# A hybrid decoder layer: four recurrent weight pairs as seven products, one scan a half, and a re-ordered out-projection

## The chip, the cores and the metric

The kernel runs on one core of a Trainium2 chip. The metric is device time in microseconds (us), the median of several executions. The engines are named as in the profile: PE (TensorE, matrix products; PEld loads its weights), DVE (VectorE), ACT (ScalarE), POOL (GpSimd) and SP (SyncE, which issues most DMAs). [...]

## The reference, cut to what matters

One layer of a decoder, 1024 tokens of 1024 features in float32. The part that the change touches, shortened:

```python
u = rms_norm(h, norm1_g)
aq, ak, av, hq, hf, hi, hg = split(u @ w_in)               # seven blocks of 512 columns
attn = rms_norm(dilated_attention(aq, ak, av), attn_norm_g)
# recurrence, 4 heads of 128: f gate, cumulated log gate per chunk, running state
forget = lb + (1 - lb) * sigmoid(f); key = 1 - forget
b = cumsum(log(forget), over the chunk)
q_dec = silu(q) * exp(b); k_inv = key * exp(-b)
o = tril(q_dec k_inv^T) iv + q_dec state;   state = exp(b_end) * state + (key * exp(b_end - b))^T iv
rec = rms_norm(o, hgrn_norm_g) * silu(hg)
h = h + concat(attn, rec) @ w_out                          # the out-projection
h = h + conv_glu(rms_norm(h, norm2_g)); out = rms_norm(h, final_norm_g)
```

## The kernel before

Feature rows lie on the 128 partitions and tokens along the free dimension, in two halves of 512 tokens. Every large product is done in split float32: an operand is a high part (a cast to the 32-bit format that PE reads fast) and a low part (the rest), and `three` (L493 to L495) issues three matmuls of 128 x 512 for each 128 x 128 block of weights: high by high, high by low, low by high.

Weights come through a `Ring`. A plan lists the pieces of weights in their order of use; each is loaded by SP into one of five raw buffers, cast by ACT (L87, `whi`) and subtracted by DVE (L89, `wlo`). At most five split pieces are alive; when a product has used one, `done` fetches the next of the plan.

The order of PE's work is written out by hand. The instructions of the other engines are ordered by a planner, from what they wait for and are wanted for, except where `pin` or `order` keeps them in program order. The hand-written order weaves two streams: dense products stand in a queue, `fill`, as generators, each of which gives 0.65 of credit for three matmuls; the recurrence, the attention and the norms call `fill.run(x)` to have x of credit of dense matmuls issued before their own next step. In the recurrent stage `play` does this by a list of `steps`, each with a due time in units of 5.2 of credit.

There are 12 recurrent weight blocks (hq, hf and hg, four heads each), taken as six pairs in the list `HG`, with both token halves. The first pair, (hf 0, hq 0), is done early, in the attention stage, as seven products instead of eight: `PairMix` forms sums of the four weight pieces on DVE, `pair_block` (L508 to L536) runs seven products of four blocks on sums of the operand (the tiles B11, B21, B22, T1 to T4) and puts their results together on DVE, with two alternating PSUM banks, "mm". Its results go to DRAM. Afterwards `restore` rebuilds the plain operand in T4's place, from x. The five other pairs are plain: `hg_block` runs for both halves and both blocks `plain_product`, 8 blocks of 3 matmuls, and `scaled` (L837) multiplies the result by the norm's factor R1.

`f_out`, `q_out` and `g_out` apply the sigmoid gates: a maximum on DVE, three ACT passes (L826 to L828), a product on DVE. `f_out` also computes B and the logarithm A (L845, L846). `recur` is one head and one half, in five steps: the scans of log gates, four of 128 columns (L935), small copies into `sm`, exponentials and products on DVE (L944 to L948); the transposes psK and the scores psA; psU and the chain of states U (L972 to L982); psO and its norm (L992 to L1001); psT and the product with the gate (L1007 to L1009). `attn_stat` and `attn_parts` norm and split the attention's output; `split_rec` splits the recurrence's.

The out-projection has, for each of the 8 blocks d of 128 output features and each half, an attention part (part 0) and a recurrent part (part 1) of four blocks each. For the first half, all the attention parts are done first, then all the recurrent parts (`out_half`); for the second half both parts of a block accumulate in one PSUM bank (`out_pair`). `square` adds up the squares for the next norm, `norm2` (L1157 on), on POOL; it is woven into the second half's products. Then the feed-forward part follows, which the change does not touch.

Of the kernel before, what the change touches and what calls it, by code (L numbers as in the profile page):

```python
# [28 lines left out]
NPAIR = 10  # L29
BIG = 1e30  # L30
# [219 lines left out]
def hybrid_kernel(ctx: ExitStack, tc: tile.TileContext, xT, w_qk, w_tok, w_hg, w_out, w_up,  # L250
# [17 lines left out]
    lb = cpool.tile([P, 96], F32, name="lb")  # L268
    epool = ctx.enter_context(pool("eps", "right"))
    eps_ = epool.tile([P, 120], F32, name="eps")  # L270
    epst, onehalf = eps_[:, 0:1], eps_[:, 64:65]
# [5 lines left out]
    R1T = rv.tile([P, P], F32, name="R1T")  # L277
    DVE.memset(ones, 1.0)
    DVE.memset(eps_[:, 0:64], EPS)
    DVE.memset(eps_[:, 64:120], 1.5)  # L280
# [21 lines left out]

    plan.extend((("V", c), tok(0, c // KS, c % KS)) for c in range(NCT))
# [4 lines left out]
    HG = [(("hf", 0), ("hq", 0)), (("hg", 0), ("hg", 1)), (("hf", 1), ("hq", 1)), (("hf", 2), ("hq", 2)),  # L308
          (("hf", 3), ("hq", 3)), (("hg", 2), ("hg", 3))]
    want_mix(HG[0], w_hg[4], w_hg[0], False)  # L310
    for pair in HG[1:]:
        for kind, h in pair:
            i = 4 * {"hq": 0, "hf": 1, "hg": 2}[kind] + h
            plan.extend((((kind, h), x), w_hg[i, :, x * H2 : (x + 1) * H2]) for x in range(2))

    def out_order(hf, d):

        return [(p, e) for p in range(2) for e in (d, d + 1)]

    def want_out(hf, d, part):  # L320
        plan.append(((("out", hf, d), part), w_out[d, :, part * H2 : (part + 1) * H2]))

    for part, d in ((x, d) for x in range(2) for d in range(NCT)):
        want_out(0, d, part)
    for d0 in range(0, NCT, 2):
        for part, d in out_order(1, d0):
            want_out(1, d, part)
# [121 lines left out]
    def rms1():  # L449
        st = bank("o", "sst")  # L450
        for hf in range(2):
            for i in range(4):
                PE.matmul(st[:, 4 * hf + i : 4 * hf + i + 1], sums[hf][:, i * P : (i + 1) * P], ones[:, 0:1], start=True, stop=True)
        tm = rv.tile([P, 64], F32, name="rst")
        rstd(R1T[:, 0:NCT], tm[:, 0:NCT], st[:, 0:NCT], 1.0 / DM)

# [203 lines left out]
    if True:  # L660
# [115 lines left out]
        def restore():  # L776
            for c in range(KS):
                x = mtile(f"x12_{c}")
                nc.sync.dma_start(x, xT[c, :, halves[1]])
                hi, lo = (y[:, c] for y in opn["T4"])  # L780
                ACT.mul(hi, x, col(V_G1 + c))
                DVE.scalar_tensor_tensor(lo, x, col(V_G1 + c), f32(hi), op0=ALU.mult, op1=ALU.subtract)

        def early_evac(m, hf, src):
            DVE.tensor_mul(src, src, R1[:, halves[hf]])
            nc.sync.dma_start(rawg[HG[0][m][0], hf], src)

        def early():

            yield from pair_block(HG[0], lambda m, hf: mtile(f"e{m}_{hf}"), early_evac)  # L790
            restore()
# [26 lines left out]
    with pool("hg", "right") as hg:  # L818
# [6 lines left out]
        def sigmoid(dst, src):  # L825
            ACT.activation(dst, src, AF.Exp, scale=-1.0)  # L826
            ACT.activation(dst, dst, AF.Ln, bias=1.0)
            ACT.activation(dst, dst, AF.Exp, scale=-1.0)  # L828

        gate, G, R2 = {}, {}, []  # L830

        def tile_of(kind, h, hf):
            tag, bufs = {"hf": ("A", 3), "hq": ("E", 4), "hg": ("GH"[h // 2], 4)}[kind]
            return ht(tag, f"{tag}{h}_{hf}", bufs)

        def scaled(x, hf, src):
            DVE.tensor_mul(x, src, R1[:, halves[hf]])  # L837
            return x

        def f_out(h, hf, A):  # L840
            B = ht("B", f"B{h}_{hf}", 3)
            DVE.tensor_scalar_max(A, A, -40.0)
            sigmoid(A, A)

            ACT.activation(B, A, AF.Identity, bias=lb[:, NG + h : NG + h + 1], scale=lb[:, 2 * NG + h : 2 * NG + h + 1])  # L845
            ACT.activation(A, A, AF.Ln, bias=lb[:, h : h + 1], scale=lb[:, NG + h : NG + h + 1])  # L846
            gate.setdefault((h, hf), {}).update(A=A, B=B)

# [7 lines left out]
        def g_out(h, hf, g_):  # L856
# [5 lines left out]

        OUT = {"hf": f_out, "hq": q_out, "hg": g_out}

        def hg_block(pair):

            for hf in range(2):
                for kind, h in pair:
                    ps = bank("mm", f"p{kind}{h}_{hf}")
                    yield from plain_product(ps, (kind, h), hf)  # L870
                    OUT[kind](h, hf, scaled(tile_of(kind, h, hf), hf, ps))

        ar = [ht("H", f"ar{x}", 4) for x in range(2)]
# [15 lines left out]
        def attn_parts(hf):  # L889
            hi, lo = spare(f"attn{hf}")  # L890
            for c in range(4):
                a = ht("F", f"as{hf}_{c}")
                nc.sync.dma_start(a, rawd[c, hf])
# [20 lines left out]
        for hf in range(2):  # L914
            for kind, h in HG[0]:
                x = tile_of(kind, h, hf)
                nc.sync.dma_start(x, rawg[kind, hf])
                OUT[kind](h, hf, x)

        AT = hg.tile([P, 4, P], F32, name="AT")  # L920
# [4 lines left out]
        def recur(h, hf):  # L925
            A, B, E = (gate[h, hf].pop(x) for x in "ABE")
            nm = f"{h}_{hf}"
            iv = hg.tile([P, 4, P], F32, tag="iv", name=f"iv{nm}", bufs=2)
# [4 lines left out]
            for c in range(4):  # L933
                s = slice(c * P, (c + 1) * P)
                DVE.tensor_tensor_scan(C[:, s], ones, A[:, s], 0.0, op0=ALU.mult, op1=ALU.add)  # L935
            sm = hg.tile([P, 12], F32, tag="sm", name=f"sm{nm}", bufs=2)
            DVE.tensor_copy(sm[:, 0:4], C3[:, :, 63])
# [679 lines left out]
```

## Time and profile before

| | |
|---|---|
| median of 3 runs | 1158.48 us (1157.97 to 1160.91) |
| the profiled execution, its own time | 1157.98 us |
| its span in the profile | 1156.2 us |
| PE busy | 1141.3 us, 6460 matmuls |
| DVE busy | 935.2 us, 1738 instructions |
| ACT busy | 572.2 us, 1121 instructions |
| attention stage with the query/key products and the early pair | about 95 to 266 us |
| the five plain recurrent pairs, with the recurrence | 266.1 to 405.8 us |
| out-projection | 405.8 to 505.4 us |
| feed-forward part and final norm | 505.4 to 1156.2 us |

A row of the timeline has the start and the length in us, the engine, the line of the kernel, the operation, what it writes and reads, its shape, and in brackets the idle time before it with what ended it. A row of a group has a count, then the busy time in us and the mean of one in ns, then the idle time before. A row of the waits has the time in all, how often and the longest. Matmuls are pipelined, so the start of the next, not the end of the last, gives what one costs.

### The profile page before, as it was taken

The numbers are of one execution on the slowest core, as the hardware profiler recorded it, in microseconds if no ns is written. First come the engines' busy times: TensorE is split into PE (matmuls) and PEld (weight loads), VectorE is DVE, ScalarE is ACT, GpSimd is POOL, SyncE is SP. The second block draws the span as 40 slices with busy tenths as digits, with TensorE's granted clock in tenths as the row PEclk, the third lists the DMA queues.
The fourth block names the chain that finished last, engine by engine and source line by source line (L and its number), as shares of the span: only waits on it lengthen the run. The fifth ranks groups of instructions, "written<-read, shape, count | busy, mean of one in ns | idle before, by whom it ended". The sixth has DMA issues, their size and how long they took to land.

```text
span 1156.2 us, 17940 instructions
## 1 busy us (share of the span) xinstructions
PE 1141.3 (99%) x6460; PEld 937.3 (81%) x6460; DVE 935.2 (81%) x1738; ACT 572.2 (49%) x1121; POOL 93.6 (8%) x111
## 2 busy tenths in 40 slices
PE   9999999999999999999999999999999999999996
PEld 7887777778788888888788888888888888888886
DVE  7676867865977886859989988888988879858987
ACT  6544454545976665546434434343344344444553
POOL 5200333320000002110000000000000000000000
PEclk9999999999999999999999999999999999999999
DMA  7225221235313253330232233223332377435532
GB/s 248 78 77 167 56 75 54 78 119 166 110 47 92 64 174 101 119 101 28 73 110 92 100 120 125 97 79 119 118 104 73 114 266 235 131 93 180 156 110 81
DMA packets 99209, 130.90 MB, mean 113 GB/s; under 512 B 25072, under 2 KB 44304, under 8 KB 99120
## 3 DMA queue, kind: packets, MB, share of 16 engines
q1 hardware_dynamic: 84832, 105.08, 29.4%
q10 hardware_dynamic: 14288, 24.67, 5.6%
q8 instruction: 51, 0.84, 0.3%
q14 instruction: 38, 0.31, 0.1%
HBM read 98.63 MB, written 31.09 MB: 112 GB/s over the span
## 4 chain that ended last, share of the span: by engine, by line
PE 89%; DVE 6%; DMA 2%; ACT 2%; issue 1%; ACTq 0%; SPq 0%; DVEq 0%
PE p L1218 11%; PE p L1216 11%; PE p L1217 11%; PE w L493 3%; PE ds L1516 3%; PE ds L1517 3%; PE ds L1515 3%; PE w L495 3%; PE w L494 3%; PE po L493 2%; PE po L494 2%; PE po L495 2%; PE da L1516 2%; PE da L1517 2%; PE da L1515 2%; PE S L706 2%
## 5 line engine op out<-in xcount | busy, mean ns | idle before, releaser
L87 ACT CAST whi<-raww 128x512 fp32r<-128x512 f32 x249 | 152.5, 618 | 223.5 <-PE p L1217 64.3
L89 DVE TENSOR_TENSOR wlo<-raww,whi 128x512 fp32r<-128x512 f32 x250 | 174.7, 700 | 37.9 <-ACT whi L87 36.1
L87 ACT CAST whi<-r 128x512 fp32r<-128x512 f32 x70 | 43.6, 623 | 85.4 <-PE ds L1516 51.4
L89 DVE TENSOR_TENSOR wlo<-r,whi 128x512 fp32r<-128x512 f32 x70 | 48.0, 687 | 19.3 <-ACT whi L87 18.9
L1517 PE MATMUL ds<-fhi,wlo 128*128 128x512 f32 x160 | 62.3, 389 | 0.0
L1516 PE MATMUL ds<-flo,whi 128*128 128x512 f32 x160 | 62.3, 389 | 0.0
L1515 PE MATMUL ds<-fhi,whi 128*128 128x512 f32 x160 | 62.2, 389 | 0.0
L1216 PE MATMUL p<-b1h,whi 128*128 128x512 f32 x160 | 62.2, 389 | 0.0
L1217 PE MATMUL p<-b1l,whi 128*128 128x512 f32 x160 | 62.2, 389 | 0.0
L1218 PE MATMUL p<-b1h,wlo 128*128 128x512 f32 x160 | 62.2, 389 | 0.0
L719 POOL TENSOR_SCALAR P<-P,st 128x128 f32<-128x128 f32 (+7 forms) x64 | 45.3, 714 | 102.7 <-DVE st L718 97.4
L1489 POOL TENSOR_TENSOR facc<-facc,sqf 128x256 f32<-128x256 f32 x2 | 1.5, 739 | 637.3 <-ACT sqf L1488 637.3
L89 DVE TENSOR_TENSOR flo<-rawf,fhi 128x512 fp32r<-128x512 f32 x70 | 48.0, 685 | 3.0 <-ACT fhi L87 3.0
L87 ACT CAST fhi<-rawf 128x512 fp32r<-128x512 f32 x70 | 43.2, 617 | 13.7 <-DMA rawf<-spT 5.2
L717 ACT ACTIVATE P<-P,st 128x128 f32<-128x128 f32 (+7 forms) x64 | 35.7, 559 | 27.2 <-DVE st L715 27.2
L1245 ACT ACTIVATE cv<-cv 128x512 f32<-128x512 f32 x44 | 27.9, 633 | 42.4 <-DVE cv L1238 42.3
L1238 DVE SCALAR_TENSOR_TENSOR cv<-g,vec,cv 128x511 f32<-128x511 f32 (+2 forms) x92 | 44.7, 492 | 4.5 <-ACT cv L1235 4.1
L1515 PE MATMUL da<-fhi,whi 128*128 128x512 f32 x120 | 46.7, 389 | 0.0
L1516 PE MATMUL da<-flo,whi 128*128 128x512 f32 x120 | 46.7, 389 | 0.0
L1517 PE MATMUL da<-fhi,wlo 128*128 128x512 f32 x120 | 46.7, 389 | 0.0
L715 DVE CUSTOM_DVE_ANT_0 P<-S,mask 128x128 f32<-128x128 f32 (+7 forms) x64 | 28.9, 487 | 9.1 <-PE S L708 7.6
L1515 PEld LDWEIGHTS ds<-fhi,whi 128*128 128x128 f32 x160 | 30.0, 188 | 6.3
(613 smaller groups left out, 3399.0 us busy)
## 6 DMA issues: line engine op xcount, KB each, us to landing
raww<-in_w_up_dram SPq DMA_DIRECT2D x88, 256.0 KB, 2.9
rawf<-spT SPq DMA_DIRECT2D x40, 256.0 KB, 2.7
r<-in_w_down_dram SPq DMA_DIRECT2D x40, 256.0 KB, 3.5
raww<-in_w_out_dram SPq DMA_DIRECT2D x32, 256.0 KB, 2.7
spB<-a ACTq DMA_DIRECT2D x30, 256.0 KB, 2.3
spT<-t ACTq DMA_DIRECT2D x30, 256.0 KB, 2.1
rawf<-spB SPq DMA_DIRECT2D x30, 256.0 KB, 2.7
raww<-in_w_hg_dram SPq DMA_DIRECT2D x24, 256.0 KB, 2.7
```

Source lines behind the costliest of these rows:

```text
L87: self.pin(self.high(hi[:, :w], raw))
L89: self.pin(low.tensor_sub(lo[:, :w], raw, f32(hi[:, :w])))
L493: PE.matmul(ps, a[0], b[0], start=start, stop=False)
L494: PE.matmul(ps, a[0], b[1], start=False, stop=False)
L495: PE.matmul(ps, a[1], b[0], start=False, stop=stop)
L719: POOL.tensor_scalar(Pt[:, :n], Pt[:, :n], st[:, 3:4], 1.0, op0=ALU.mult, op1=ALU.mult)
L1216: PE.matmul(ps, hi[:, s], bhi, start=(start and n == 0), stop=False)
L1217: PE.matmul(ps, hi[:, s], blo, start=False, stop=False)
L1218: PE.matmul(ps, lo[:, s], bhi, start=False, stop=(stop and n == len(rhs) - 1))
L1515: PE.matmul(ps[d], hi[:, s], ahi, start=(k == 0), stop=False)
L1516: PE.matmul(ps[d], hi[:, s], alo, start=False, stop=False)
L1517: PE.matmul(ps[d], lo[:, s], ahi, start=False, stop=(k == NPAIR - 1))
```

## The change

1. The middle four recurrent pairs, (hg 0, hg 1), (hf 1, hq 1), (hf 2, hq 2) and (hg 2, hg 3), are done as seven products with `PairMix` and `pair_block`; the last, (hf 3, hq 3), stays plain. `restore` moves from the end of the early pair to just ahead of that last pair.
2. The gates of the early pair are computed in the attention stage, before the results go to DRAM. B and the logarithm of the gate are computed in `recur`, and the gate of hg is held back until the step of psO (`g_now`).
3. In `recur` one scan of 512 columns, with a factor tile `chunks` that is zero at each chunk's start, takes the place of four; the copies into `sm` fall away (three small exponentials read the strided columns instead of one); the product on psU goes from DVE to four ACT multiplications.
4. The out-projection is a list of blocks: first the attention part of both halves for d below 4, which share a split weight piece, with the first half's attention part for the others; then the first half's recurrent part; then the rest of the second half's attention part, and its recurrent part. Each is a product of its own, added to `h_`. The second half's squares are added on DVE.
5. `attn_parts` and `restore` load through the ring's raw buffers; due times and buffer counts are new; a few small constant tiles are narrower.

```diff
+SHARED = 4
...
     HG = [(("hf", 0), ("hq", 0)), (("hg", 0), ("hg", 1)), (("hf", 1), ("hq", 1)), (("hf", 2), ("hq", 2)),
-          (("hf", 3), ("hq", 3)), (("hg", 2), ("hg", 3))]
+          (("hg", 2), ("hg", 3)), (("hf", 3), ("hq", 3))]
...
+    for pair in HG[1:-1]:
+        want_mix(pair, w_of(*pair[0]), w_of(*pair[1]), False)
+    plan.extend(((key, x), w_of(*key)[:, x * H2 : (x + 1) * H2]) for key in HG[-1] for x in range(2))
+    OUT_BLOCKS = [[(hf, 0, d) for d in range(NCT) for hf in range(2) if d < SHARED or hf == 0], [(0, 1, d) for d in range(NCT)],
+                  [(1, 0, d) for d in range(SHARED, NCT)] + [(1, 1, d) for d in range(NCT)]]
...
         def early_evac(m, hf, src):
             DVE.tensor_mul(src, src, R1[:, halves[hf]])
+            F = otile1(f"F{hf}") if m else src
+            DVE.tensor_scalar_max(F, src, -40.0)
+            sigmoid(F, F)
+            if m:
+                DVE.tensor_mul(src, src, F)
             nc.sync.dma_start(rawg[HG[0][m][0], hf], src)
...
         def hg_block(pair):
+            def evac(m, hf, src):
+                DVE.tensor_mul(src, src, R1[:, halves[hf]])
+                OUT[pair[m][0]](pair[m][1], hf, src)
+            return pair_block(pair, lambda m, hf: tile_of(*pair[m], hf), evac)
...
+        def restore():
+            for c in range(KS):
+                hi, lo = (y[:, c] for y in opn["T4"])
+                x = ring.raw(xT[c, :, halves[1]])
+                ACT.mul(hi, x, col(V_G1 + c))
+                DVE.scalar_tensor_tensor(lo, x, col(V_G1 + c), f32(hi), op0=ALU.mult, op1=ALU.subtract)
+        def dense():
+            for pair in HG[1:-1]:
+                yield from hg_block(pair)
+            restore()
+            yield from plain_block(HG[-1])
...
         def recur(h, hf):
+            ACT.activation(B, A, AF.Identity, ...)
+            ACT.activation(A, A, AF.Ln, ...)
...
-            for c in range(4):
-                s = slice(c * P, (c + 1) * P)
-                DVE.tensor_tensor_scan(C[:, s], ones, A[:, s], 0.0, op0=ALU.mult, op1=ALU.add)
-            sm = hg.tile([P, 12], F32, tag="sm", name=f"sm{nm}", bufs=2)
-            DVE.tensor_copy(sm[:, 0:4], C3[:, :, 63])
-            DVE.tensor_copy(sm[:, 4:8], C3[:, :, 127])
-            DVE.tensor_sub(sm[:, 8:12], sm[:, 4:8], sm[:, 0:4])
+            DVE.tensor_tensor_scan(C, chunks, A, 0.0, op0=ALU.mult, op1=ALU.add)
...
-            order(ACT.activation(ex, sm, AF.Exp))
-            DVE.tensor_sub(A3, C3, sm[:, 0:4].unsqueeze(2).to_broadcast([P, 4, P]))
+            DVE.tensor_sub(A3, C3, C3[:, :, 63:64].to_broadcast([P, 4, P]))
+            order(ACT.activation(ex[:, 8:12], A3[:, :, 127], AF.Exp))
+            order(ACT.activation(ex[:, 0:4], C3[:, :, 63], AF.Exp))
+            order(ACT.activation(ex[:, 4:8], C3[:, :, 127], AF.Exp))
...
-            DVE.tensor_mul(U[:, :n], psU[:, : n * P]..., ex[:, 8 : 8 + n]...)
+            for c in range(n):
+                ACT.mul(U[:, c], psU[:, c * P : (c + 1) * P], ex[:, 8 + c : 9 + c])
...
+            g_now(h, hf)
             psO = bank("o", f"psO{nm}")
...
-        N = len(HG[1:]) * UNIT
+        N = 3.5 * (len(HG) - 2) + 4.0
...
-        for (h, hf), start, at in (((0, 0), 2.2, 4.3), ((0, 1), 5.3, 7.1), ((1, 0), 8.1, 9.9), ((1, 1), 10.9, 12.7),
-                                   ((2, 0), 13.7, 15.5), ((3, 0), 16.5, 18.3), ((2, 1), 19.3, 21.1), ((3, 1), 22.1, 23.9)):
+        for (h, hf), start in zip(((0, 0), (0, 1), (1, 0), (1, 1), (2, 0), (3, 0), (2, 1), (3, 1)),
+                                (1.9, 5.1, 8.2, 11.3, 14.4, 17.5, 20.4, 23.3)):
+            at = start + 1.9
             steps += zip((start, at, at + 1, at + 2.2, at + 3.8), rec_steps(h, hf))
...
-            steps.append((12.6 + 5.6 * hf, lambda hf=hf: attn_ops.update({hf: attn_parts(hf)})))
+            steps.append(((14.5, 16.3)[hf], lambda hf=hf: attn_ops.update({hf: attn_parts(hf)})))
...
+        def out_block(hf, part, d):
+            key = out_key(hf, part, d)
+            hi, lo = ring.get(key)
+            x = None if part else residual(hf, d)
+            ps = bank(next(out_banks), f"po{part}_{hf}_{d}")
+            ...
+            DVE.tensor_add(h, ps, h if part else x)
+            if part:
+                square(hf, d)
...
-                    POOL.tensor_add(accs[hf], accs[hf], sq)
+                    (DVE if hf else POOL).tensor_add(accs[hf], accs[hf], sq)
...
-        fill.add(*[out_half(part, d) for part in range(2) for d in range(NCT)])
-        play(22.15)
+        fill.add(*[out_block(*x) for x in OUT_BLOCKS[0]])
+        play(25.0)
         split_rec(0)
-        play(N + 8)
-        fill.run()
+        fill.add(*[out_block(*x) for x in OUT_BLOCKS[1] + OUT_BLOCKS[2][: NCT - SHARED]])
+        play(28.5)
+        while steps:
+            steps.pop(0)[1]()
         split_rec(1)
...
-    fill.add(*[out_pair(1, d) for d in range(0, NCT, 2)])
-    fill.run(6.0)
+    fill.add(*[out_block(1, 1, d) for d in range(NCT)])
+    out_banks = cycle(("mm", "mm", "s", "o"))
+    fill.run(2.5)
     with pool("n2", "left") as n2p:
-        weave(norm2(0), 37.5, 2)
+        weave(norm2(0), 13.9, 2)
```

More of the change, by code (lines that the diff above doesn't have):

```diff
@@ L2 @@
 from contextlib import ExitStack
-from itertools import islice
+from itertools import cycle
 import concourse.bass as bass
@@ L306, in hybrid_kernel, with out_key @@
         want_mix(("qk", p), w_qk[2 * p], w_qk[2 * p + 1], True)
-    HG = [(("hf", 0), ("hq", 0)), (("hg", 0), ("hg", 1)), (("hf", 1), ("hq", 1)), (("hf", 2), ("hq", 2)),
-          (("hf", 3), ("hq", 3)), (("hg", 2), ("hg", 3))]
[L310 to L327, printed above, removed]
+    want_mix(HG[0], w_of("hf", 0), w_of("hq", 0), False)
+    for pair in HG[1:-1]:
[3 more added lines that the diff above has]
+                  [(1, 0, d) for d in range(SHARED, NCT)] + [(1, 1, d) for d in range(NCT)]]
+    def out_key(hf, part, d):
+        return (("out", 0 if part == 0 and d < SHARED else hf, d), part)
+    for x in sum(OUT_BLOCKS, []):
+        if out_key(*x) == (("out", x[0], x[2]), x[1]):
+            plan.append((out_key(*x), w_out[x[2], :, x[1] * H2 : (x[1] + 1) * H2]))
     def part(f, i):
@@ L774, in values, with sigmoid @@
             nc.sync.dma_start(rawd[p, hf], ot)
[L776 to L782, printed above, removed]
+        def sigmoid(dst, src):
+            ACT.activation(dst, src, AF.Exp, scale=-1.0)
+            ACT.activation(dst, dst, AF.Ln, bias=1.0)
+            ACT.activation(dst, dst, AF.Exp, scale=-1.0)
         def early_evac(m, hf, src):
             DVE.tensor_mul(src, src, R1[:, halves[hf]])
+            F = otile1(f"F{hf}") if m else src
[3 more added lines that the diff above has]
+                DVE.tensor_mul(src, src, F)
             nc.sync.dma_start(rawg[HG[0][m][0], hf], src)
@@ L870, in hg_block @@
                     yield from plain_product(ps, (kind, h), hf)
-                    OUT[kind](h, hf, scaled(tile_of(kind, h, hf), hf, ps))
-        ar = [ht("H", f"ar{x}", 4) for x in range(2)]
+                    x = tile_of(kind, h, hf)
+                    DVE.tensor_mul(x, ps, R1[:, halves[hf]])
+                    OUT[kind](h, hf, x)
+        def restore():
[9 more added lines that the diff above has]
+            yield from plain_block(HG[-1])
+        ar = []
         def attn_stat(hf):
@@ L1027, in weave @@
             fill.run()
-        fill.add(*[hg_block(pair) for pair in HG[1:]])
-        UNIT = 4.0
-        N = len(HG[1:]) * UNIT
+        fill.add(dense())
+        N = 3.5 * (len(HG) - 2) + 4.0
         steps = []
@@ L1085, in hybrid_kernel @@
         accs = {}
-        def out_product(ps, hf, d, part, start, stop):
-            key = ("out", hf, d)
-            hi, lo = ring.get((key, part))
-            m = (rec_parts if part else attn_ops)[hf]
+        def out_block(hf, part, d):
[3 more added lines that the diff above has]
+            ps = bank(next(out_banks), f"po{part}_{hf}_{d}")
             for c in range(4):
                 s = slice(c * P, (c + 1) * P)
-                three(ps, (hi[:, s], lo[:, s]), [x[:, c] for x in m], start and c == 0, stop and c == 3)
-                if c == 3:
-                    ring.done((key, part))
+                three(ps, (hi[:, s], lo[:, s]), [y[:, c] for y in (rec_parts if part else attn_ops)[hf]], c == 0, c == 3)
+                if c == 3 and not (hf == 0 and part == 0 and d < SHARED):
+                    ring.done(key)
                 yield 0.65
+            h = h_[:, d, halves[hf]]
+            DVE.tensor_add(h, ps, h if part else x)
+            if part:
+                square(hf, d)
+        out_banks = cycle(("mm",))
         def square(hf, d):
```

81 lines of the change are left out of this document (35 added, 46 removed).

## The prediction

> **What bounds the kernel now.** I read the page first, then the waits of the tensor engine, then its order of time around the longest wait, then the stretches.
>
> ```profile
> span 1156.2 us, 17940 instructions
> PE 1141.3 (99%) x6460; PEld 937.3 (81%) x6460; DVE 935.2 (81%) x1738; ACT 572.2 (49%) x1121; POOL 93.6 (8%) x111
> PE   9999999999999999999999999999999999999996
> DVE  7676867865977886859989988888988879858987
> PEclk9999999999999999999999999999999999999999
> PE 89%; DVE 6%; DMA 2%; ACT 2%; issue 1%; ACTq 0%; SPq 0%; DVEq 0%
> ```
>
> TensorE (PE) is busy in every slice at the full granted clock, and the chain that ended last is 89% PE. VectorE (DVE) is second at 81%. So a matmul less is time less, as long as no other engine makes PE wait. It hardly waits now:
>
> ```profile
> PE psK L954 <- DVE B L948: 2.8, 1, 2.8
> PE w L493 <- ACT u L521: 1.0, 1, 1.0
> PE po L493 <- DVE H L837: 0.3, 1, 0.3
> ```
>
> Those and two shorter ones at the start are all the waits of note. The longest, in order of time, followed by the starts of the recurrent weight products and of the out-projection:
>
> ```profile
> 289.38 0.39 PE L493 MATMUL phf<-B11h,whi 128*128 128x512 f32 x1
> 289.61 0.39 PE L494 MATMUL phf<-B11l,whi 128*128 128x512 f32 x1
> 289.83 0.39 PE L495 MATMUL phf<-B11h,wlo 128*128 128x512 f32 x1
> 293.01 0.63 PE L954 MATMUL psK<-ident,B 128*128 128x128 f32 x4 [2.79 <-DVE B L948]
> ...
> 266.11 0.50 PE L493 MATMUL phg<-B11h,whi 128*128 128x512 f32 x1
> 405.83 0.39 PE L493 MATMUL po<-attn0h,whi 128*128 128x512 f32 x1
> ```
>
> Two facts: a 512-column matmul starts every 0.227 us (289.38, 289.61, 289.83) although one lasts 0.39; and the stretch that the change rewrites, the five plain pairs, runs from 266.1 to 405.8, 139.7 us. What the engines do around it, in windows (length, then PE, PEld, DVE, ACT, POOL busy):
>
> ```profile
> 228.00:262.00 34.00, 34.00 (x426) 27.13 (x427) 23.34 (x70) 17.43 (x44) 8.78 (x15) 1.00 0.34 105
> 266.00:290.00 24.00, 24.00 (x111) 19.67 (x107) 12.35 (x32) 14.62 (x27) 0.00 (x0) 1.00 0.51 159
> 290.00:406.00 116.00, 113.21 (x639) 94.18 (x639) 92.16 (x201) 86.24 (x205) 1.80 (x3) 1.00 0.26 78
> 290.00:319.00 29.00, 26.21 (x148) 20.98 (x148) 27.18 (x60) 26.46 (x59) 1.21 (x1) 1.00 0.35 110
> 406.00:464.00 58.00, 57.67 (x314) 48.21 (x314) 43.27 (x81) 32.52 (x84) 8.60 (x7) 1.00 0.43 136
> 468.00:492.00 24.00, 24.00 (x108) 19.79 (x107) 21.62 (x31) 13.81 (x24) 4.76 (x3) 1.00 0.38 121
> ```
>
> From 266 to 406 DVE works 12.35 + 92.16 = 104.5 of 140 us, ACT 100.9. This is the room the change spends.
>
> **The change, part by part.** *Matmuls removed.* A plain pair is 4 products of 8 column blocks, each 3 matmuls: 96. Seven products of 4 blocks are 84. Four pairs: 48 matmuls x 0.227 = 10.9 us off PE. The out-projection keeps its 32 products of 4 blocks, since only weights are shared.
>
> *The first wait.* psK waits 2.79 us for B. In the 16 us before, ScalarE (ACT) is filled with the sigmoids of the early pair, queued ahead of the recurrence's own exponentials:
>
> ```profile
> 277.67 0.64 ACT L826 ACTIVATE A<-A 128x512 f32<-128x512 f32 x1 [1.25 <-DVE A L842]
> ...
> 290.86 0.61 ACT L946 ACTIVATE A<-A 128x512 f32<-128x512 f32 x1
> ```
>
> The change computes these (12 ACT operations of 0.62, four maxima and two products on DVE) in the attention stage, and holds the gates of hg back until `g_now`. The new first recurrence is issued at 1.9 units and its psK at 3.8 (5.2 of credit each, 0.65 of credit per three matmuls): 9.9 and 19.8 of credit, so about 276.5 and 286.9 us. Its chain (two ACT of 0.81, scan 1, difference 0.69, two exponentials 1.24, two products 1.38) is 5.9 us against 10.4 of cover. I take the whole 2.8, bounds 0 and 2.8; the 0.3 of the out-projection's start goes in neither direction.
>
> *Where those operations land.* In 228 to 262 ACT has 16.6 us idle and DVE 10.7, against 7.4 and 3.1 added: 0. If queue order spoiled that, the bound is one more wait like the 2.8.
>
> *DVE in the stretch*, the part that can give the gain back. Durations:
>
> ```profile
> L89 DVE TENSOR_TENSOR wlo<-raww,whi 128x512 fp32r<-128x512 f32 x19 | 13.0, 686 | 3.7 <-ACT whi L87 3.5
> L935 DVE TENSOR_TENSOR_SCAN C<-ones,A 128x128 f32<-128x128 f32 x32 | 11.8, 408 | 0.9 <-ACT A L846 0.9
> L981 DVE SCALAR_TENSOR_TENSOR U<-U,ex 128x128 f32<-128x128 f32 x15 | 5.2, 344 | 0.2
> L972 DVE TENSOR_TENSOR U<-psU,ex 128x512 f32<-128x512 f32 x4 | 2.7, 683 | 0.0
> L937 DVE COPY sm<-C 128x4 f32<-128x4 f32 x7 | 1.2, 165 | 0.0
> L894 DVE SCALAR_TENSOR_TENSOR as<-as,vec,R 128x512 f32<-128x512 f32 x6 | 4.5, 750 | 4.5 <-DMA as<-raw 4.4
> L982 ACT ACTIVATE st<-U,ex 128x128 f32<-128x128 f32 x17 | 6.4, 398 | 7.0 <-DVE U L972 4.5 <-DVE U L977 1.4 <-DVE U L981 1.1
> ...
> 292.78 1.29 DVE L89 TENSOR_TENSOR wlo<-raww,whi 128x512 fp32r<-128x512 f32 x2
> 282.86 1.36 DVE L935 TENSOR_TENSOR_SCAN C<-ones,A 128x128 f32<-128x128 f32 x4
> ```
>
> One full-width operation lasts 0.69 but two in a row take 1.29, so 0.60 each back to back. Per pair the seven products add 4 sums of weights, 3 more low parts (7 for 4) and 7 sums of products: 14 x 0.60 = 8.4, four pairs 33.6 us. The early pair takes 3.1 off. Per recurrence the product on psU (0.68 or 0.55) goes to ACT, three tiny operations of 0.16 go, and four scans of 1.36 together become one. That single scan has no row: between 0.75 (0.408 plus the 0.34 that full width costs over 128 columns in L89 against L981) and 1.36; I take 1.0. So 1.5 per recurrence, some six of them: 8 to 9. Recurrences start every 3.1 units instead of 2.8 and there are 18 units instead of 20, so one recurrence (about 6 of DVE, 5 of PE) leaves the stretch. The second half's attention parts come in whole: 3. Sum 104.5 + 33.6 - 3.1 - 8.5 - 6 + 3 = 123.5 us of busy time as now packed; with more back to back perhaps 118. PE needs 139.7 - 10.9 - 2.8 - 5 = 121. DVE goes from 75% to about 98% of it.
>
> [...]
>
> What that does to PE: between 290 and 319 DVE was 94% busy and PE lost the 2.8; slices of the page exist where DVE shows 9 and PE loses nothing. If DVE can be filled to 94% only, 118 of work takes 125.5, so PE waits 4.5; at 98% nothing; with 123.5 of work at 94%, 10. I take 4, bounds 0 and 10. Most exposed are the pairs hf1/hq1 and hf2/hq2 (a bank of two must be emptied each 2.72 us, beside a recurrence) and the last plain pair, beside attn_parts and the restoring of T4.
>
> *ACT*: 3 more casts and a copy per pair (16 x 0.62 = 9.9), four multiplications of 0.4 for psU and two more tiny exponentials per recurrence (6 x 2 = 12), less 7.4 and one recurrence (10): 105 of 121, so it has room: 0. Between psU and psO lie 1.2 units, 6.5 us; the chain grows by 0.9.
>
> *DMA and the SyncE queue*: restore and attn_parts now take a raw buffer of the ring, 12 loads, so the weight loads queue behind them for a buffer and the casts behind those. Weights are five entries ahead, 13 us, and a weight lands in 2.7 us: 0, at worst one 2.5 us wait as L894 has now. Four weight loads and their splits fall away, eight additions (0.60) come with the separate halves; from 406 to 464 DVE is 43.27 of 58: 0. The fill runs out at 24.0 units, with psO of (2, 1) due at 24.5, 3.8 us after its psU for a chain of about 4: 0 to 1.
>
> *norm2 of the first half.* Its 16 operations on DVE run under the last out-projection blocks:
>
> ```profile
> 468.12 0.40 PE L373 MATMUL ss<-acchi,ones 128*128 128x512 f32 x1
> 488.79 1.78 DVE L1165 SCALAR_TENSOR_TENSOR uf<-h,vec,r2y 128x512 f32<-128x512 f32 x1
> 491.26 0.69 DVE L1168 TENSOR_TENSOR b1l<-uf,b1h 128x512 fp32r<-128x512 f32 x1
> 488.47 1.55 POOL L1108 TENSOR_TENSOR acc<-acc,sq 128x512 f32<-128x512 f32 x1 [3.22 <-ACT sq L1106]
> 505.37 0.39 PE L1216 MATMUL p0g<-b1h,whi 128*128 128x512 f32 x1
> ```
>
> Now 23.8 us to the last b1l, against 37.2 to the product that reads it. After: 26 of credit remain behind ss (176.8 in all less 150.8), 27.2 us, and DVE must do 18 operations for norm2, 10 additions from PSUM, 7 sums of squares that POOL did, about 9 low parts: 44 x 0.61 = 27. The 1.78 beside POOL's 1.55 falls back to 0.75, since these sums leave POOL; that is inside the 27. I take 1 us of waiting, bounds 0 and 4.
>
> *Sum*: -10.9 - 2.8 + 4 + 1 = -8.7. The profiled execution took 1157.98 (span 1156.2 and 1.8 around it), 0.5 below the median of 1158.48: 1157.98 - 8.7 = 1149.3, say 1149.
>
> **The rivals.** *Clean*: the planner keeps DVE full and PE waits under 2 us. For it: slices with DVE at 9 and no PE loss. Against: recurrences arrive in lumps. 1157.98 - 13.7 + 1 = 1145. *DVE is the bound*: 123.5 of work at 94%, 10, plus norm2's 4: 1157.98 - 13.7 + 14 = 1158, no change. For it: window 290 to 319. Against: sums of squares and gates can slip. *Slower*: evacuation pays at every product. A pair of PSUM banks gives each product 2.72 us until its bank is wanted; an addition behind a recurrence's scan, difference and two products (about 3 us) comes too late. At a mean wait of 0.49 us for each of the 28 products the 13.7 is gone; at 0.7 it costs 20 and gives 1164. For it: products 5 and 7 need three dependent additions. Against: the same block in the attention stage, with DVE at 23.34 of 34, shows no wait on a DVE addition. *The early sigmoids do not free the first wait*: 1152.
>
> **How the numbers follow.** Forecast (waits of 3 to 8 us, 1147 to 1153) 0.53, clean 0.22, first wait kept 0.06, DVE bound 0.11, slower 0.08. Below about 3.5 us (0.3%) a difference cannot be told from none: the DVE case is mostly there, and the forecast is faster throughout: faster 0.80, same 0.11, slower 0.09. The range goes from the clean case with its best scan, 1143.5, to 1156, leaving out the bound and the slower case.
>
> **What would show it.** The count of PE matmuls falls by 48; psK's wait on B at the first recurrence is gone; the recurrent stretch shows DVE above 90%; PE's waits name DVE's additions (L523 to L535 of now) or low parts, a few us together; p0g starts soon after the last b1l. I am wrong if PE's waits exceed 8 us in the stretch, if weight loads wait for raw buffers, or if they stay under 2 us.

## The result, and the profile after

The changed kernel takes 1152.7 us (median of 6 runs, 1151.81 to 1153.63) where the kernel before takes 1159.25 (6 runs, 1157.97 to 1160.91): a ratio of 0.9943, 95% interval 0.993 to 0.9956. It is faster by 6.5 us: 3.7 us above the forecast of 1149, and inside the range. Its profiled execution took 1153.45 us, 4.5 below that of before, where the sum had 8.7.

The page of the changed kernel: span, busy times, the slices of PE and DVE, the chain that ended last.

```profile
span 1151.7 us, 17921 instructions
PE 1138.9 (99%) x6412; PEld 929.6 (81%) x6412; DVE 960.3 (83%) x1748; ACT 586.8 (51%) x1177; POOL 87.8 (8%) x107
PE   9999999999999999999999999999999999999996
DVE  7685877768999975889989989888988789857987
PE 94%; DVE 3%; ACT 1%; DMA 1%; issue 0%; SPq 0%; ACTq 0%; DVEq 0%
```

There are 48 matmuls fewer, as forecast, and PE is still the bound, 94% of the chain instead of 89%. Yet PE's busy time fell by 2.4 us only, and 48 x 0.227 are 10.9. What PE waited for, every row of that view:

```profile
PE warm L420 <- DVE eps L281: 1.1, 1, 1.1
PE w L492 <- ACT u L520: 0.9, 1, 0.9
PE w L492 <- ACT whi L88: 0.7, 1, 0.7
PE v L492 <- DVE whi L88: 0.3, 1, 0.3
PE p0g L1233 <- DVE h L1128: 0.2, 1, 0.2
```

The wait of psK for B (2.8 us before) is gone. The 1.1, the 0.9 and the 0.3 were there before, at the same places and about as long. In the recurrent stretch PE waited once, 0.7 us. The row names a cast, but that matmul also needs a PSUM bank, which the second of two subtractions at the fifth product of `pair_block` (L530) frees:

```profile
287.33 0.68 DVE L530 TENSOR_TENSOR G<-G,w 128x512 f32<-128x512 f32 x1
288.16 0.47 PE L492 MATMUL w<-B22h,whi 128*128 128x512 f32 x1 [0.68 <-ACT whi L88]
```

L530 ends at 288.01, 0.15 us ahead of the matmul. Ten of the profiles (this one, and nine of the experiments below) have a wait at this matmul. In all ten PE starts 0.14 to 0.15 us after the end of L530, while the rows name a cast in seven, `ar` in one and L530 itself in two. So PE waited for `pair_block`'s arithmetic on DVE, as the prediction had it, but for 0.7 us and not for a few. The gain wasn't lost in waits. The windows (length, then PE, PEld, DVE, ACT, POOL busy, granted clock) of the recurrent stretch, of 29 us in it, and of the last out-projection blocks with norm2:

```profile
270.40:394.10 123.70, 123.02 (x655) 100.61 (x652) 115.72 (x213) 95.77 (x232) 2.45 (x2) 1.00 0.39 119
290.00:319.00 29.00, 29.00 (x163) 23.74 (x163) 27.55 (x49) 21.04 (x52) 2.16 (x1) 1.00 0.38 113
475.00:499.00 24.00, 24.00 (x104) 19.34 (x103) 23.73 (x39) 12.56 (x23) 0.00 (x0) 1.00 0.28 88
```

and a window of 140 us around the recurrent stretch of before:

```profile
266.00:406.00 140.00, 137.21 (x749) 113.85 (x746) 104.51 (x232) 100.86 (x231) 1.80 (x3) 1.00 0.30 92
```

DVE went from 75% of the stretch to 93.5%, and the stretch from 139.7 us to 123.7. That is 16 us less, where the prediction had 18.7 for PE alone (down to 121). In the 29 us from 290 on, where DVE had been 94% busy and PE had lost 2.8, DVE is now 95% busy and PE loses nothing (other work lies there now: this stretch begins 4.3 us later than before's).

One small term can be read off directly: the single scan, all eight of them (min, median, max in ns):

```profile
L964 DVE TENSOR_TENSOR_SCAN C<-chunks,A x8: 1211/1217/1226, 281.7 to 428.4; 128x512 f32<-128x512 f32 x8
```

It takes 1.22 us; I had taken 1.0, and the four scans it replaces took 1.36 together.

Where the missing microseconds are shows in the order of time. The first matmul of `i` (the second of the two value products, `v` and `i`) and the first of `w` (the seven-product pairs), before:

```profile
51.24 0.49 PE L493 MATMUL i<-whi,B11h 128*128 128x512 f32 x1
94.90 0.39 PE L493 MATMUL w<-B11h,whi 128*128 128x512 f32 x1
```

and after, with the first of the out-projection and of the feed-forward part (405.83 and 505.37 in the rows of before that the prediction shows):

```profile
53.89 0.48 PE L492 MATMUL i<-whi,B11h 128*128 128x512 f32 x1
98.50 0.40 PE L492 MATMUL w<-B11h,whi 128*128 128x512 f32 x1
394.06 0.40 PE L492 MATMUL po<-attn0h,whi 128*128 128x512 f32 x1
500.11 0.47 PE L1233 MATMUL p0g<-b1h,whi 128*128 128x512 f32 x1 [0.23 <-DVE h L1128]
```

At 98.50 us the changed kernel is already 3.6 us behind, in value products that the change doesn't touch at all, at the same granted clock of 1.00 and with no wait that would explain it. Two things add up there. The first is the start. The fourth and fifth value product, before:

```profile
6.67 0.39 PE L493 MATMUL v<-whi,B11h 128*128 128x512 f32 x1
6.90 0.39 PE L494 MATMUL v<-wlo,B11h 128*128 128x512 f32 x1
```

and after:

```profile
7.00 0.63 PE L492 MATMUL v<-whi,B11h 128*128 128x512 f32 x1
7.43 0.63 PE L493 MATMUL v<-wlo,B11h 128*128 128x512 f32 x1
```

The first twelve take 3.7 us before and 5.4 after, because ten of them lie 0.43 us or more apart instead of two. This goes with the execution and not with the kernel: the profiles of `e2`, `e5` and `e8` below have it too, and those of the other nine don't. What sets it isn't shown (the granted clock reads 1.00 in it); it takes 1.7 us, and the six times of the kernel after do lie in two groups that far apart, 1151.81 to 1151.96 and 1153.45 to 1153.63 us. The other 1.9 us are single matmuls that got slower. Part of the value products of the changed kernel:

```profile
45.08 0.39 PE L494 MATMUL v<-whi,B22l 128*128 128x512 f32 x1
...
46.44 0.40 PE L494 MATMUL v<-whi,B22l 128*128 128x512 f32 x1
46.67 0.39 PE L492 MATMUL v<-whi,B21h 128*128 128x512 f32 x1
...
48.07 0.39 PE L492 MATMUL v<-whi,B21h 128*128 128x512 f32 x1
```

From 45.08 to 46.44 lie six steps: 0.227 us each, with B22. From 46.67 to 48.07 lie six as well: 0.233 each, with B21. Same operation, same shape, the same ring of weight pieces `whi` and `wlo`; only the operand's tile is another. In the out-projection the steps are 0.235 (four rows in the experiments below). Over the trace, split 512-column matmuls that read B11, B21, T2, T4, the attention's or the recurrence's split pieces or, in the feed-forward part, the pieces `ahi` and `alo` run at 0.232 to 0.235 in the median, and the others (T1, T3, B22, nearly all of the feed-forward part) at 0.227 to 0.229. That is 288 in the value products, 432 in `w`, 72 in the plain pair, 384 in the out-projection and 72 later: 1248 matmuls times 0.005 to 0.008, 6 to 10 us (an estimate).

What can have done this is the one item of the change that I priced at nothing, the narrower constants: `lb` went from 96 columns to 16 and `eps` from 120 to 16. By the sides and the order in which the kernel opens its pools, the tiles of the weights ring stand behind `lb` at one end of the on-chip memory, and the operand tiles named above stand at the other end, behind `eps`; B22, T1, T3 and the feed-forward operands stand on the ring's side. (Two more tiles were narrowed, `R1T` and `rst`; they are allocated behind the operand tiles.) Narrower constants move the two groups against each other, here by 4 x (216 - 32) = 736 bytes in each partition.

### The profile page after: what moved, and what is told of

It is laid out like the page before. It is cut to its first block, busy times and chain, and to the rows that moved or that the text cites. A ratio compares the mean times of both kernels' runs of the same rounds, so it can differ in the third digit from the quotient of the medians.

```text
span 1151.7 us, 17921 instructions
## 1 busy us (share of the span) xinstructions
PE 1138.9 (99%) x6412; PEld 929.6 (81%) x6412; DVE 960.3 (83%) x1748; ACT 586.8 (51%) x1177; POOL 87.8 (8%) x107
## 4 chain that ended last, share of the span: by engine, by line
PE 94%; DVE 3%; ACT 1%; DMA 1%; issue 0%; SPq 0%; ACTq 0%; DVEq 0%
PE p L1235 11%; PE p L1234 11%; PE p L1233 11%; PE w L492 5%; PE w L493 4%; PE w L494 4%; PE ds L1532 3%; PE ds L1533 3%; PE ds L1534 3%; PE po L492 3%; PE po L493 3%; PE po L494 2%; PE da L1533 2%; PE da L1532 2%; PE da L1534 2%; PE S L705 2%
## 5 line engine op out<-in xcount | busy, mean ns | idle before, releaser
L88 ACT CAST whi<-raww 128x512 fp32r<-128x512 f32 x257 | 157.6, 618 | 224.4 <-PE p L1234 78.1
L90 DVE TENSOR_TENSOR wlo<-raww,whi 128x512 fp32r<-128x512 f32 x258 | 179.7, 699 | 33.1 <-ACT whi L88 31.3
L90 DVE TENSOR_TENSOR wlo<-r,whi 128x512 fp32r<-128x512 f32 x70 | 47.8, 684 | 19.2 <-ACT whi L88 18.3
L1534 PEld LDWEIGHTS ds<-fhi,wlo 128*128 128x128 f32 x160 | 30.0, 188 | 6.3
```

What stands on the lines that cost most here:

```text
L88: self.pin(self.high(hi[:, :w], raw))
L90: self.pin(low.tensor_sub(lo[:, :w], raw, f32(hi[:, :w])))
L1534: PE.matmul(ps[d], lo[:, s], ahi, start=False, stop=(k == NPAIR - 1))
```

## The experiments

Theories at this point: **placement** (where the constants leave the tiles sets the pitch of the matmuls, that is the time from start to start, and that cost some 5 us), and its rivals: **new work** (something else in the changed code slows PE) and, for the recurrent stretch, **slack** (DVE still has room) against **full** (DVE has none, whatever PE's waits say). Times are medians; each ratio is to the kernel before, timed on the same chip.

**1. One constant wider, in the kernel after** (`e1_eps24`)

```diff
-    eps_ = epool.tile([P, 16], F32, name="eps")
+    eps_ = epool.tile([P, 24], F32, name="eps")
```

> The changed kernel with one constant tile (eps, the first of the right-hand pools) 24 columns wide instead of 16, so that every tile of pool ub, which lies behind it, starts at a multiple of 64 bytes again, as before the change; nothing else differs. Address theory: the 512-column matmuls that read B11, B21, T2, T4, attn and rec go from 0.233-0.235 back to 0.227 us; about 1224 of them (288 in the v and i products, 432 in w, 72 in the plain pair, 384 in the out-projection, 48 at the end) x 0.007 = 8.6 us less: 1144 us. Rival (the slower pitch belongs to the change's own traffic on the other engines, or to the chip that day): the pitch stays at 0.234 and the time within 1 us of the changed kernel's 1152.7.

1150.84 us, ratio 0.9932 (0.9919 to 0.9946). Eight columns of a constant that nothing reads are worth 1.9 us by the medians and 1.3 by the ratios, whose intervals overlap; 8.6 had been expected. The value products fell to 0.229, the out-projection only to 0.233.

**2. The kernel before, with the narrow constant** (`e2_before_eps16`)

```diff
-    eps_ = epool.tile([P, 120], F32, name="eps")
-    epst, onehalf = eps_[:, 0:1], eps_[:, 64:65]
+    eps_ = epool.tile([P, 16], F32, name="eps")
+    epst, onehalf = eps_[:, 0:1], eps_[:, 8:9]
```

> The kernel before with only this tile narrowed from 120 to 16 columns, so that ub's tiles start 32 bytes past a multiple of 64. Address theory: the same matmuls take 0.234 instead of 0.227; about 1320 of them (288 v and i, 240 w, 360 in five plain pairs, 384, 48) x 0.007 = 9.2 us more: about 1168 us. Rival: no change, 1158.5 to 1159.5.

1166.17 us, ratio 1.0065 (1.0048 to 1.0083): 7.3 us slower. Its page has the same instructions as the kernel before, and 10.3 us more of PE (1.7 of them are the slow start described above):

```profile
span 1164.6 us, 17940 instructions
PE 1151.6 (99%) x6460; PEld 939.3 (81%) x6460; DVE 934.7 (80%) x1738; ACT 572.5 (49%) x1121; POOL 94.7 (8%) x111
```

This rules out **new work** as the source: the loss appears with none of the change's code.

**3. Both constants at 24 columns** (`e3_eps24_lb24`), to test the first rule that I had for it, that a tile must start on a multiple of 64 bytes

```diff
-    lb = cpool.tile([P, 16], F32, name="lb")
+    lb = cpool.tile([P, 24], F32, name="lb")
...
-    eps_ = epool.tile([P, 16], F32, name="eps")
+    eps_ = epool.tile([P, 24], F32, name="eps")
```

> As e1_eps24, and the tile lb, the last of the left-hand constants, 24 columns wide instead of 16: the ring of weights and every later left-hand tile (T1, T3, B22, the feed-forward operands) start 32 bytes past a multiple of 64, while ub stays aligned. Address theory: nearly every 512-column matmul has one such operand, some 4380 x 0.007 = 31 us more than e1: about 1175 us; where both operands are off the cost is either 7 or 14 ns, which the rows of w on T1 against w on B11 will tell. Rival (only the right-hand pools matter, or only the operand that is loaded as weights): 1144 us, or less than half of the 31.

1153.17 us, ratio 0.9953 (0.9937 to 0.9969). The rule is wrong: the edit moved the ring and the feed-forward operands together off their multiple, and the feed-forward products kept 0.227, where 1175 us had been expected. Not where a tile stands counts, then, but how tiles stand to each other. The next theory: the distance between the two operands of a matmul.

**4 to 6. Three ways to set that distance** (`e5_eps72`, `e6_lb72`, `e7_eps8`), each against the kernel after

```diff
# e5
-    eps_ = epool.tile([P, 16], F32, name="eps")
+    eps_ = epool.tile([P, 72], F32, name="eps")
# e6
-    lb = cpool.tile([P, 16], F32, name="lb")
+    lb = cpool.tile([P, 72], F32, name="lb")
# e7
-    eps_ = epool.tile([P, 16], F32, name="eps")
-    epst, onehalf = eps_[:, 0:1], eps_[:, 8:9]
+    eps_ = epool.tile([P, 8], F32, name="eps")
+    epst, onehalf = eps_[:, 0:1], eps_[:, 4:5]
```

> The changed kernel with eps 72 columns wide instead of 16. The first three runs refute a rule of 64 bytes for one operand alone: e1 got 1.9 us of the 8.6, and only in the v and i products, and e3 shifted every left-hand tile without slowing the products whose two operands both lie on the left. New theory: what counts is the distance between the tile that is loaded as weights and the tile that streams, modulo a power of two; before the change it was a multiple of 2048 bytes for every pair of tiles (ring against ub), after it 736 more, in e1 704, in e2 416, in e3 672. Here it is 512. If 512 is the period, all pitches go back to 0.227 and the time to about 1144 us; if the period is 1024 or 2048, it stays at 1151 to 1153.

> The changed kernel with lb 72 columns wide instead of 16 and eps as changed: the same distance of 512 as e5_eps72, but reached by moving the left-hand tiles, so that ub's tiles stay 32 bytes past a multiple of 64. Distance theory: the same time as e5_eps72 within 1 us. Rival (the right-hand tiles' own address counts, as 512-byte or 64-byte steps): no better than the changed kernel, 1152 to 1153.

> The changed kernel with eps 8 columns wide: the distance is 768, a multiple of 256 but not of 512. If the period is 256 or less: about 1144 us. If it is 512 or more: as e1, 1150 to 1153.

1146.98, 1146.89 and 1147.01 us; ratios 0.99 (0.9883 to 0.9917), 0.9901 (0.9881 to 0.9921) and 0.9903 (0.988 to 0.9926). All three put the median of each of these products back to 0.227. The second moves only the ring's side and leaves the other operands where the kernel after has them; the first and third move only the other side, one up, one down. So it is the distance between the two sides. The out-projection at 480 us, in the kernel after:

```profile
479.88 0.40 PE L494 MATMUL po<-rec1h,wlo 128*128 128x512 f32 x1
480.12 0.40 PE L492 MATMUL po<-rec1h,whi 128*128 128x512 f32 x1
480.35 0.40 PE L493 MATMUL po<-rec1l,whi 128*128 128x512 f32 x1
480.59 0.40 PE L494 MATMUL po<-rec1h,wlo 128*128 128x512 f32 x1
```

and with `eps` at 8 columns:

```profile
480.18 0.39 PE L494 MATMUL po<-rec1h,wlo 128*128 128x512 f32 x1
480.41 0.39 PE L492 MATMUL po<-rec1h,whi 128*128 128x512 f32 x1
480.64 0.39 PE L493 MATMUL po<-rec1l,whi 128*128 128x512 f32 x1
480.86 0.39 PE L494 MATMUL po<-rec1h,wlo 128*128 128x512 f32 x1
```

Three steps take 0.71 us in the first and 0.68 in the second. The medians give back 5.7 us and the ratios 4.6. The spans give back 6.5 (1151.7 to 1145.2), of which 1.7 is the slow start of the one profile; so the placement is worth about 5 us here, less than the 6 to 10 reckoned above and than the 8.6 expected. The stages of that kernel (`eps` at 8) start at

```profile
51.31 0.47 PE L492 MATMUL i<-whi,B11h 128*128 128x512 f32 x1
94.96 0.39 PE L492 MATMUL w<-B11h,whi 128*128 128x512 f32 x1
388.91 0.39 PE L492 MATMUL po<-attn0h,whi 128*128 128x512 f32 x1
493.58 0.47 PE L1233 MATMUL p0g<-b1h,whi 128*128 128x512 f32 x1 [0.77 <-DVE h L1128]
```

The untouched stages are back at before's times (the start is the same in both profiles), and p0g starts 11.8 us earlier than before. From here on this kernel is the base for the experiments on the change itself.

**7. A seventh distance** (`e12_eps40`): period 256 bytes or 128?

```diff
-    eps_ = epool.tile([P, 16], F32, name="eps")
+    eps_ = epool.tile([P, 40], F32, name="eps")
```

> The changed kernel with eps 40 columns wide: the distance between the ring and ub is 640, a multiple of 128 but not of 256. Period of 128 bytes: 0.227 us a matmul and 1147.0, as e5, e6 and e7. Period of 256: 0.229 to 0.234 and about 1151, as e1 (704, a multiple of 64 but not of 128).

1151.55 us, ratio 0.993 (0.9909 to 0.9951). 640 is a multiple of 128, and the pitch of the two-sided products is 0.232, where 512 and 768 have 0.227: so not 128, and 256 fits what was run. All widths together; the pitch is the median of start to start over all matmuls of the kind, in us, for the value products apart by the side on which their operand stands:

| kernel | columns of lb + eps | bytes narrower than before | of these mod 256 | value products, B11, B21, T4 | value products, B22 | out-projection |
|---|---|---|---|---|---|---|
| before | 96 + 120 | 0 | 0 | 0.227 | 0.227 | 0.227 |
| before, eps 16 | 96 + 16 | 416 | 160 | 0.232 | 0.232 | 0.234 |
| after | 16 + 16 | 736 | 224 | 0.234 | 0.227 | 0.235 |
| eps 24 | 16 + 24 | 704 | 192 | 0.229 | 0.227 | 0.233 |
| lb 24, eps 24 | 24 + 24 | 672 | 160 | 0.231 | 0.232 | 0.234 |
| eps 40 | 16 + 40 | 640 | 128 | 0.232 | 0.227 | 0.232 |
| eps 72 | 16 + 72 | 512 | 0 | 0.227 | 0.227 | 0.227 |
| lb 72 | 72 + 16 | 512 | 0 | 0.227 | 0.227 | 0.227 |
| eps 8 | 16 + 8 | 768 | 0 | 0.227 | 0.227 | 0.227 |

The column of B22 shows that the theory isn't complete. B22 and the ring stand on the same side, and with `eps` narrowed in the kernel before neither of them moved; yet their products slowed as well, there and in the other kernel at 160. So the distance between the two sides decides, but not only through the two operands of one matmul. What else plays a part stays open.

**8. DVE's savings taken back** (`e4_scans_U_on_DVE`, against `eps` at 24): does the stretch have the room that PE's missing waits suggest?

```diff
-            DVE.tensor_tensor_scan(C, chunks, A, 0.0, op0=ALU.mult, op1=ALU.add)
+            for c in range(4):
+                s = slice(c * P, (c + 1) * P)
+                DVE.tensor_tensor_scan(C[:, s], ones, A[:, s], 0.0, op0=ALU.mult, op1=ALU.add)
...
-            for c in range(n):
-                ACT.mul(U[:, c], psU[:, c * P : (c + 1) * P], ex[:, 8 + c : 9 + c])
+            DVE.tensor_mul(U[:, :n], psU[:, : n * P].rearrange(...), ex[:, 8 : 8 + n]...)
```

> As e1_eps24, with two parts of the change undone in the recurrence: four scans of 128 columns instead of one of 512, and the product on psU on VectorE again instead of four ScalarE multiplications. Per recurrence 0.14 + 0.6 us more on VectorE, six in the stretch. Theory (VectorE has slack where PE waits for it, though it is 94% busy): within 1 us of e1_eps24. Rival (my predicted term: VectorE is at its limit, each us of it is waited for): 4 us more than e1.

1153.8 us, ratio 0.9961 (0.9946 to 0.9976): 3.0 more than its base on the same chip, and DVE's busy time in the stretch grew by 2.9 (115.5 to 118.4). **Slack** (within 1 us) is wrong. Its waits now name the arithmetic of `pair_block`:

```profile
PE w L492 <- DVE A L523: 1.1, 1, 1.1
...
PE w L492 <- DVE H L522: 0.4, 1, 0.4
PE w L492 <- DVE E L526: 0.3, 1, 0.3
```

**9 and 10. DVE loaded by measure** (`e8_dve_10us`, `e9_dve_19us`, against `eps` at 8): one or two maxima of a tile with itself, 0.60 us each, at each of 16 seven-product results

```diff
+                for _ in range(1):   # e9: range(2)
+                    DVE.tensor_tensor(src, src, src, op=ALU.max)
```

> As e7_eps8 (1147.0), with one more full-width VectorE operation (the maximum of a tile with itself, 0.60 us) behind each of the 16 evacuating products of the four seven-product pairs: 9.6 us more VectorE work in the stretch, in the chain to the gates, nothing else changed. Slack theory: VectorE has about 8 us idle in the 124 us of the stretch, so PE waits 2 us more: 1149. Rival (VectorE is already what PE runs by, as e4 gave 3.0 us for about 4.4 of work): 0.68 of each us: 1153.5. Second rival (the operations are not on a path that PE waits for): 1147.

> As e8, with two such operations each: 19.2 us more. Slack theory: 11 us more than e7: 1158. Rival: 13: 1160. Second rival: below 1150.

1153.89 us, ratio 0.995 (0.9935 to 0.9965), and 1165.74, ratio 1.0053 (1.0038 to 1.0068), where the base has 1147.01. So 9.6 us on DVE cost 6.9, and 19.2 cost 18.7 (by the ratios, since the base ran on another chip, 5.4 and 17.4). The second is above all that was expected (1158 and 1160). The recurrent stretch of the base, of the first and of the second:

```profile
266.10:389.00 122.90, 122.04 (x655) 100.61 (x652) 115.68 (x213) 95.61 (x232) 2.46 (x2) 1.00 0.39 119
```
```profile
266.00:396.00 130.00, 125.86 (x696) 101.78 (x691) 125.44 (x230) 97.85 (x233) 3.36 (x2) 1.00 0.36 112
```
```profile
266.00:407.00 141.00, 127.02 (x658) 101.89 (x654) 132.80 (x241) 97.74 (x230) 1.82 (x2) 0.98 0.32 101
```

DVE is 94.1%, 96.5% and 94.2% busy in the three. The second window begins 2 us ahead of its stretch, since that profile has the slow start. From its first matmul to the first of the out-projection the stretch takes 122.7, 128.0 and 141.2 us: 5.3 more for the first 9.6 us on DVE, and some 13 more for the second. In the last, PE loses 14 of 141 us, and the longest of its waits are for the arithmetic at L526, L522 and L523:

```profile
PE w L492 <- DVE E L526: 5.3, 2, 3.2
PE w L492 <- DVE H L522: 2.3, 1, 2.3
PE w L492 <- DVE A L523: 1.8, 1, 1.8
PE phf L492 <- DVE A L882: 1.6, 1, 1.6
```

Two things beside DVE's load are in the 13. The granted clock: its record reads 0.5 for 6.8 us, from 305.9 us on, around the longest wait (3.2 us, ending at 307.1), and PE is busy for 5.6 of them. The matmuls lie 0.43 us apart there (307.70 and 308.13) instead of 0.227, which makes up to 2.8 us (an estimate). And the order of work: DVE itself stands idle for 8 of the 141 us while PE loses 14, so it isn't only that DVE is full; results behind the extra work come too late for their bank, as the prediction's slower rival describes. How much each took isn't shown. **Full** is therefore right in sense and not in measure: at 94% DVE took about half of 9.6 us more without PE paying for it.

**11. The early gates back in the recurrent stage** (`e10_gates_late`, against `eps` at 8)

```diff
-            F = otile1(f"F{hf}") if m else src
-            DVE.tensor_scalar_max(F, src, -40.0)
-            sigmoid(F, F)
-            if m:
-                DVE.tensor_mul(src, src, F)
...
-                gate.setdefault((h, hf), {})["EA"[kind == "hf"]] = x
+                OUT[kind](h, hf, x)
```

> As e7_eps8, with the early pair's gates (four maxima and two products on VectorE, 12 ScalarE passes) computed again behind the attention stage, ahead of the first recurrence, as before the change. Theory (the first wait of 2.8 us went because this work left ScalarE's queue there): psK or the products around it wait 2 to 3 us more: 1149 to 1150. Rival (it went because the gates of hg are held back and the steps start earlier or later): within 0.5 us of 1147.0.

1150.7 us, ratio 0.9924 (0.991 to 0.9939): 3.7 us by the medians, 2.4 by the ratios, whose intervals overlap (the base ran on another chip). In the traces the stretch takes 126.0 us instead of 122.7, 3.3 more. The base's one wait in the stretch (0.9) is gone and there is a new one:

```profile
288.13 0.47 PE L492 MATMUL w<-B11h,whi 128*128 128x512 f32 x1 [2.56 <-ACT ar L900]
288.79 0.63 PE L494 MATMUL w<-B11h,wlo 128*128 128x512 f32 x1
289.22 0.63 PE L492 MATMUL w<-B11h,whi 128*128 128x512 f32 x1
```

That is 1.7 us of waits more. The row names `ar`, but here too PE starts 0.15 us after the subtraction that frees its bank (L532, done at 287.98). It came late: from 279.5 us to there DVE had work without a gap, part of it the early pair's gates, ahead of it. The other 1.6 us come behind the wait: from 288.5 to 291.9 the granted clock is 0.50, and the matmuls lie 0.43 us apart (289.22 against 288.79). So with the gates late about the same is lost as in the 2.8 of before, but in another place and to another operation; psK itself doesn't wait. That the early gates alone took the wait at psK away isn't shown.

**12. The pair (hg 2, hg 3) plain again** (`e11_hg23_plain`, against `eps` at 8)

```diff
-    for pair in HG[1:-1]:
+    for pair in HG[1:-2]:
...
+            yield from plain_block(HG[-2])
```

> As e7_eps8, with the pair (hg 2, hg 3) plain again instead of seven products: 12 matmuls more, x 0.227 = 2.7 us, against 8.4 us less on VectorE. Theory (PE sets the time): 1149.7. Rival (VectorE's relief gives it back): 1147 to 1148, or less.

1149.89 us, ratio 0.9919 (0.9902 to 0.9935): 2.9 us by the medians, 1.9 by the ratios, for 12 matmuls (6424 instead of 6412), which the prediction prices at 12 x 0.227 = 2.7. The forecast for this was 1149.7. A pair less of DVE's extra work gives nothing back here; one pair more of seven products pays in full.

## Why the prediction was right, and where it wasn't

The time, the sign and the range held; the mechanism held in part. The matmuls went as forecast, the wait at psK is gone, and DVE is above 90% in the stretch. But the forecast's 1149 rests on waits of 3 to 8 us behind DVE's arithmetic, and PE waited 0.7 us in the stretch, 0.9 with the tiles well placed. That is under the 2 us which the prediction itself names as a sign of being wrong. A cost that it didn't have filled the place. Term by term:

- *Matmuls, -10.9.* Right. 48 are gone, and the single pair tried cost about its 2.7 us when undone.
- *The first wait, -2.8.* Right in size: it is gone, and with the early gates put back the stretch is 3.3 us longer, though by a wait in another place. The cause is shown only so far.
- *DVE in the stretch, +4 (0 to 10).* Too dear by 2 to 3 us, though by the right reckoning. I had worked out 118 us of DVE work, at most 94% of a stretch to be filled, 121 us needed by PE. Measured with the tiles well placed: 115.7 us of work, 94.1% filled, 122.0 us needed by PE, 122.9 us of stretch. The mis-sized step is the work (118 to 123.5 forecast, 115.7 measured), not the share: experiments 8 to 10 show that the next microseconds of DVE cost PE between half of themselves and the whole, and those after them more. So the condition of the clean rival (under 2 us of waits) was met, but its reason, that DVE can be kept full at no cost, was not: PE and DVE end together here.
- *The scan at 1.0.* It is 1.22; on six recurrences 1.3 us of DVE more, inside the 115.7.
- *norm2, +1 (0 to 4).* Right in size, not in cause: p0g waits 0.2 us in the kernel after and 0.8 with the tiles well placed, for an addition of the out-projection (L1128). The last b1l is done at 491.5 us, 8.6 ahead of p0g, so p0g didn't wait for norm2's result. That norm2's work on DVE made the addition late is likely, with DVE busy for 23.73 of 24 us in the window quoted above, but not shown.
- *ACT, weight loads and the SyncE queue at 0.* Right: the one wait whose row names a cast was for L530.
- *The narrower constants, at nothing.* This is the step that failed. It wasn't costed; it sat in a half sentence of the change. By experiments 4 to 6 it costs 5.7 us by the medians (1152.7 against 1147.01; by the ratios, 0.9943 against 0.9903, 4.6).
- *A reading.* Of the "two shorter ones at the start" among the waits of before, one is 1.1 us (`warm`), longer than two of the three shown; it is the same after and changes no term.

With the last step mended the change gains 11.7 us: -10.9 - 2.8 and about 2 us of waits. p0g shows the same, 11.8 us earlier. That is between the clean rival's 1145 and the forecast's 1149. The forecast of 1149 thus came near 1152.7 with one error of some 2 to 3 us on the dear side and one of some 5 on the cheap side, and that they offset each other is luck. The best kernel of the runs is the changed one with the two constants at 16 + 72, 72 + 16 or 16 + 8 columns: 1147.0 us, 1% faster than before.

## What to carry to other kernels

A change of a small tile's size can move other tiles and cost time in stages that read them, here 5.7 us by the medians: compare the start-to-start time of matmuls in a stage that the change does *not* touch before reading anything into the stage that it does. An engine for which PE waits 0.7 us in 124 may still have little room: at 94% busy, DVE passed on about half of the next 9.6 us and more than all of the 9.6 after that. A row of the waits names what ended last by the profile: see whether the same wait in another run names something else, and what frees the bank that the matmul writes. And compare the first matmuls of two profiles before taking the difference of their spans. And where the profile gives a share to which an engine can be filled, the forecast is as good as the count of its work, so count that closest.

## What the runs showed of the hardware

Not expected: in these runs the pitch of a split 512-column matmul went with how far the tiles at the two ends of the on-chip memory stand apart. At the distance of before, or one changed by 512 or 768 bytes in the partition, it is 0.227 us; changed by 416, 640, 672, 704 or 736 bytes it is 0.229 to 0.235 for matmuls with one operand from each end, 1 to 3.5% more, at a granted clock of 1.00 and with no wait shown. It shows both ways round: the value products load the operand tile as weights and stream the ring's, the out-projection does the reverse, and at 736 bytes they take 0.234 and 0.235. The value products with B22, both of whose operands stand at one end, slow down at 416 and 672 bytes (0.232 in the median), in part at 640 (mean 0.229), and not at 704 and 736; the feed-forward products that stand at that end alone kept 0.227 in the kernel after (736) and in `e3` (672). A change of 256 bytes itself was not run. Why 0, 512 and 768 bytes, all multiples of 256, are the fast ones of those run, why B22 slows at some of the distances, and why the value products recover more than the out-projection at 704, stays open.

In `e10` a wait of PE cost more than its length: behind its 2.6 us the granted clock was 0.50 for 3.4 us, with the matmuls 0.43 us apart. Around the wait of 3.2 us in `e9` it was 0.50 for 6.8 us; behind the 2.8 at psK in the kernel before it stayed at 1.00. What decides isn't shown.

Plain float32 took PE longer than the split format: in the kernel before, the four 128-column products of psU (L970) take 0.81 us to the start of the next matmul (300.21 to 301.02), where a 512-column matmul of split pieces starts every 0.227, three of them in 0.68.
